# Where the gate row of layer 1's experts is applied, and the order of the last combine

## The chip, the cores and the metric

The kernel runs on one core of a Trainium2 chip. The metric is the time of one execution on the device, in microseconds (us). The program is given three times, and the median counts. The engines are PE (TensorE: matmuls, and PEld for its weight loads), DVE (VectorE), ACT (ScalarE), POOL (GpSimd) and SP (SyncE, which issues transfers here). Each works through its own instructions in order, and semaphores hold them against each other.

## What is computed

The model has an attention block, then a second block of two layers, each with a mixer and a mixture of experts. The change concerns the experts of the last layer, layer 1. There are 512 token rows of 1024 numbers (`h`, normed and modulated), 16 experts (4 groups of 4) with 256 hidden columns, and each token goes to two experts. Cut to what matters:

```python
def hier_moe(h, wg, bg, we, be, w_gate, w_up, w_down):
    ...                                   # combine: weights of the two chosen experts of each token
    for g in range(MOE_GROUPS):
        a = jnp.einsum('nd,edf->nef', h, w_gate[g])
        u = jnp.einsum('nd,edf->nef', h, w_up[g])
        hid = jax.nn.silu(a) * u * combine[:, g, :, None]
        out = out + jnp.einsum('nef,efd->nd', hid, w_down[g])
    return out
...
f_l = hier_moe(modulate(x, norm_ffn[i], mod_l[3], mod_l[4]).reshape(B * S, D), *moe_p)
x = x + mod_l[5] * f_l.reshape(B, S, D)
```

`mod_l[5]` is a row of 1024 numbers, the same for every token: the gate. Everything is fp32.

## The kernel before

`moe` runs a layer's experts. For layer 1 `n` is 4 (four tiles of 128 tokens). Each expert is a block `b` of up to `CAP` = 96 token rows; an expert with more rows would need further blocks, which stand in a branch (`tc.If`, label `rest1`, line 1974) that all engines jump over here.

**One block** (`block`, from line 1809). POOL gathers the token rows from DRAM by an indirect DMA (line 1780, tile `xg`). PE transposes them (`tr`, line 201); ACT rounds the result to `xhi` and DVE takes the rest `xlo` (line 157). The expert's weights come as six tiles of 128x1024 (512 KB each, tile `wraw`), which SP loads (line 138). Each tile is split in two: ACT casts it to `whi` (line 145) and DVE subtracts to get `wlo` (line 146). Every product is three matmuls, `whi` by `xhi`, `wlo` by `xhi` and `whi` by `xlo` (`mm3`, lines 151 to 153). Four tiles make `gu`, the gate and up products, from which ACT and DVE make `hd` (lines 1840, 1841); it is transposed and split, and two tiles make the two 512-wide halves of the output in PSUM (`yo`). These two halves are multiplied by the gate on DVE (line 1860, `y<-yo,g`). POOL scatters `y` to DRAM (line 1790): `yD` has two rows for each token, one for each of its two experts. In layer 0, `n` is 6, the blocks have 128 rows, there is no gate in `block`, and ACT copies `yo` to `y` (line 1858) instead.

**The order.** Blocks are interleaved by `run`: a block's transposes and first products are written between the parts of the block before. `prepare` puts a gather two blocks ahead, and with it `index_expert` (lines 1762 to 1772), DVE and PE work that finds the rows of that block. The tile framework then orders each engine's instructions by priority and dependence. The weight tiles turn through a ring of 25 buffers (14 + 4 + 7), so a load waits until the split of the tile 25 places earlier is done. `y` has 2 buffers, `yo` 2, the split tiles 4.

**The last two blocks** (`LAST`, 14 and 15) are not scattered. Their gated `y` is split into `hi` and `lo` in two `wraw` buffers (line 157, `wraw<-y`), and PE adds them to the tokens by a 0/1 matrix `sh` (`product`, lines 2015 and 2016, tile `yb`). Rows of `yD` that only these blocks would write are set to zero early: ACT makes a zero `y` (line 2006), and POOL scatters it twice.

**The end.** `run(None, None)` and `end()` finish blocks 14 and 15. SP loads the first rows of `yD` for four token tiles, and POOL adds the second rows in four accumulating DMAs (line 2045). DVE then adds `yb` to the residual `x` (line 2052, `X<-X,yb`) for two tiles, adds their `ys` (line 2055), and does the same for the other two; `finish` stores each 512-wide half from ACT's queue (line 130).

Of the kernel before, what the change touches and what calls it, by code (L numbers as in the profile page):

```python
# [8 lines left out]
F32 = mybir.dt.float32  # L9
# [5 lines left out]
OP = mybir.AluOpType  # L15
# [4 lines left out]
P = 128  # L20
# [875 lines left out]
class Fill:  # L896
# [10 lines left out]
    def finish(self):  # L907
        for _ in self.todo:
            pass
# [494 lines left out]
def row_bcast(K, st, pool, l, r, m, name):  # L1404
    t = pool.tile([P, D], F32, name=name, tag=name)
    K.load(t, st["dram"][l][r:r + 1, m * D:(m + 1) * D].to_broadcast([P, D]))
    return t
# [300 lines left out]
def moe(K, st, l, toks, mo, keep, first_ring, finish):  # L1708


    tc, nc, small, io, V = K.tc, K.nc, K.small, K.io, K.nc.vector
    n = len(toks)
# [4 lines left out]
    LAST = range(NLAST[l], 16)  # L1717
# [10 lines left out]
    pp = K.pool(es, "moep", PSUM)  # L1728
    yD = K.dram.tile([n * P, 2, D], F32, name="yD%d" % l)
# [9 lines left out]
    def source(e, i):  # L1739
        return io["ew"][l, e, i] if isinstance(e, int) else io["ew"][l, bass.ds(e, 1), i].rearrange("o p c -> (o p) c")  # L1740

    def fetch(m):
        for _ in range(min(m, len(chunks))):
            b, i = chunks.pop(0)
            ready[b, i] = K.fetch(source(expert[b], i))
# [37 lines left out]
    ysc, back, gate = [], [], None  # L1783
    half = (slice(0, 512), slice(512, 1024))
    if n == 4:
        gate = row_bcast(K, st, ex, l, toks[0][2], 5, "g5")

    def scatter(b, y):
        c = y.shape[0]
        sc = nc.gpsimd.indirect_dma_start(out=yD.rearrange("t k d -> (t k) d"),  # L1790
                                          out_offset=bass.IndirectOffsetOnAxis(ap=idx[:c, b:b + 1].bitcast(U32), axis=0),
                                          in_=y, in_offset=None, bounds_check=2 * n * P - 1, oob_is_err=False)
        for o in ysc:
            tc.declare_no_dep(sc.ins, o.ins, reason="other rows")
        ysc.append(sc)

    def block(b, e, xg):

        c = CAP if b < 16 else P
        xg = xg[:c]  # L1800
        xT = [ex.tile([P, KT, P], F32R, name=q, tag=q, bufs=2)[:, :, :c] for q in ("xhi", "xlo")]
        for k0 in range(0, KT, 4):
            tp = pp.tile([P, 512], F32, name="tr", tag="tr", bufs=2)
            for k in range(4):
                K.transpose(tp[:, k * c:(k + 1) * c], xg[:, (k0 + k) * P:(k0 + k + 1) * P])
            done = K.split(xT[0][:, k0:k0 + 4], xT[1][:, k0:k0 + 4], tp[:, :4 * c].rearrange("p (k q) -> p k q", k=4))

        def split(k):

            q, i = flow[k]  # L1810
            with ExitStack() as b_es:
                for x in done if q == 0 and i >= HOLD0 else ():
                    b_es.enter_context(tc.issue_after(x.ins))
                parted[q, i] = K.halves(ready.pop((q, i)))
            fetch(1)

        def weights(i):

            if b not in expert:
                K.load(xgs[2], source(e, i))  # L1820
                K.split(*spare, xgs[2])
                return spare
            k = flow.index((b, i))
            for q in range(k, min(k + 1 + SPLIT_AHEAD, len(flow))):
                if flow[q] not in parted:
                    split(q)
            return parted[b, i]

        yield
        gu = pp.tile([P, 512], F32, name="gu", tag="gu", bufs=2)[:c]  # L1830
        for kp in range(4):
            if kp == 2:
                yield
            hi, lo = weights(kp)
            for j in range(2):
                k = 2 * kp + j
                K.mm3(gu, (xT[0][:, k], xT[1][:, k]), (hi[:, j * 512:(j + 1) * 512], lo[:, j * 512:(j + 1) * 512]),
                      k == 0, k == KT - 1)
        hd = ex.tile([P, 256], F32, name="hd", tag="hd", bufs=2)[:c]
        nc.scalar.activation(hd, gu[:, :256], AF.Silu)  # L1840
        V.scalar_tensor_tensor(hd, hd, wsl[:c, b:b + 1], gu[:, 256:], op0=OP.mult, op1=OP.mult)
        yield
        tp = pp.tile([P, 512], F32, name="tr", tag="tr", bufs=2)
        for k in range(2):
            K.transpose(tp[:, k * c:(k + 1) * c], hd[:, k * P:(k + 1) * P])
        hT = [ex.tile([P, 2, P], F32R, name=q, tag=q, bufs=2)[:, :, :c] for q in ("hhi", "hlo")]
        K.split(hT[0], hT[1], tp[:, :2 * c].rearrange("p (k q) -> p k q", k=2))
        yield
        y = ex.tile([P, D], F32, name="y", tag="y", bufs=2)[:c]
        for ch in range(2):  # L1850
            hi, lo = weights(4 + ch)
            ps = pp.tile([P, 512], F32, name="yo", tag="yo", bufs=2)[:c]
            for j in range(2):
                K.mm3(ps, (hT[0][:, j], hT[1][:, j]), (hi[:, j * 512:(j + 1) * 512], lo[:, j * 512:(j + 1) * 512]),
                      j == 0, j == 1)
            cc = slice(ch * 512, (ch + 1) * 512)
            if gate is None:
                nc.scalar.copy(y[:, cc], ps)  # L1858
            else:
                V.tensor_tensor(y[:, cc], ps, gate[:c, cc], op=OP.mult)  # L1860
        if b not in LAST:
            return scatter(b, y)
        sh = token_rows(b, c)
        if gate is None:
            hi, lo = [K.wsp.tile([P, D], F32R, name=nm, tag=nm)[:c] for nm in ("whi", "wlo")]
        else:
            hi, lo = [K.raw(F32R)[:c] for _ in range(2)]
        for cc in half:
            K.split(hi[:, cc], lo[:, cc], y[:, cc])
        back.append((sh, hi, lo))  # L1870

    def token_rows(b, c):

        tok = small.tile([P, 1], F32, name="sk", tag="sk", bufs=2)[:c]
        V.tensor_copy(tok, xidx[:c, b:b + 1])
        V.tensor_scalar(tok, tok, -2048.0, None, op0=OP.add)
        at = small.tile([P, 8], F32, name="sa", tag="sa", bufs=2)[:c, :n]
        V.tensor_scalar(at, K.tile256[:c, :n], -0.5, tok, op0=OP.mult, op1=OP.add)
        sh = (K.wsp if gate is None else ex).tile([P, KT * P], F32R, name="sh", tag="whi" if gate is None else "xhi",
                                                  bufs=None if gate is None else 2)  # L1880
        sh = sh.rearrange("p (k q) -> p k q", q=P)[:c, :n]
        V.tensor_tensor(sh, K.iota[:c, None, :].to_broadcast([c, n, P]), at[:, :, None].to_broadcast([c, n, P]),
                        op=OP.is_equal)
        return sh
# [3 lines left out]
    def run(b, e, xg=None):  # L1888


        new = block(b, e, xg) if b is not None else None
        for x in (new, behind.pop(0) if len(behind) > 1 else None, new, behind[0] if behind else None, new):
            if x is not None:
                next(x, None)
        if new:
            behind.append(new)

    def end():
        next(behind.pop(), None)
# [112 lines left out]
    def product(t, psums):  # L2012
        for ps, cc in zip(psums, half):
            for i, (sh, hi, lo) in enumerate(back):
                nc.tensor.matmul(ps, sh[:, t], hi[:, cc], start=i == 0, stop=False)
                nc.tensor.matmul(ps, sh[:, t], lo[:, cc], start=False, stop=i == len(back) - 1)

    if n == 6:
        g5, ys = {}, {}
# [20 lines left out]
        es.close()  # L2040
        return load, combine
    run(None, None)
    ys = {t: K.fetch(yD[t * P:(t + 1) * P, 0]) for t, x, r in toks}
    for t, x, r in toks:
        nc.gpsimd.dma_start(ys[t], yD[t * P:(t + 1) * P, 1], accum_op=OP.add)
    end()
    for p in range(0, n, 2):
        for t, x, r in toks[p:p + 2]:
            psums = [pp.tile([P, 512], F32, name="yb", tag=tag, bufs=2) for tag in ("yo", "gu")]
            product(t, psums)  # L2050
            for ps, cc in zip(psums, half):
                V.tensor_add(x[:, cc], x[:, cc], ps)  # L2052
        for t, x, r in toks[p:p + 2]:
            for cc in half:
                V.tensor_add(x[:, cc], x[:, cc], ys[t][:, cc])  # L2055
                finish(t, x, cc)
    es.close()
    K.rings = base

# [339 lines left out]
def body(nc, tc, io, out, stop=None, skip1=False, force_slow=False):  # L2399
    with ExitStack() as es:  # L2400
# [79 lines left out]
        h_es.close()  # L2480
        a_es.close()
        back = moe(K, st, 0, toks, mo, keep, ring, None)
        if stop == "xb0":
            dump(X, C)
# [34 lines left out]
```

## Time and profile before

| | |
|---|---|
| three runs, median (lowest to highest) | 1970.19 us (1966.07 to 1971.62) |
| the profiled execution | 1971.35 us |
| its span, first to last instruction | 1969.5 us |
| mean granted TensorE clock | 0.947 |
| PE, PEld, DVE busy over the span | 91%, 70%, 71% |
| ACT, POOL busy over the span | 49%, 18% |
| layer 1's experts, from the branch to the end | about 1758 to 1969.5 us |

A time in the rows further down is us from the first instruction. A line of a timeline gives the start, the length, the engine, the line, the operation and the tiles (written<-read); `x2` merges two in a row. In square brackets stands how long the engine was idle before it, and what ended the wait. A matmul's end is modelled, so a busy PE is not PE at its peak. A line of waits says which instruction waited for which, with the sum, the count and the longest wait.

### The profile page before, as it was taken

The numbers are of one execution on the slowest core, as the hardware profiler recorded it, in microseconds if no ns is written. First come the engines' busy times: TensorE is split into PE (matmuls) and PEld (weight loads), VectorE is DVE, ScalarE is ACT, GpSimd is POOL, SyncE is SP. The second block draws the span as 40 slices with busy tenths as digits, with TensorE's granted clock in tenths as the row PEclk, the third lists the DMA queues.
The fourth block names the chain that finished last, engine by engine and source line by source line (L and its number), as shares of the span: only waits on it lengthen the run. The fifth ranks groups of instructions, "written<-read, shape, count | busy, mean of one in ns | idle before, by whom it ended". The sixth has DMA issues, their size and how long they took to land. (4 is left out here: it accounts for less than half of the span.)

```text
span 1969.5 us, 27283 instructions
## 1 busy us (share of the span) xinstructions
PE 1787.4 (91%) x9504; PEld 1371.1 (70%) x9504; DVE 1401.3 (71%) x2764; ACT 969.6 (49%) x1855; POOL 358.7 (18%) x301
## 2 busy tenths in 40 slices
PE   6999999899999997899989999699969799968996
PEld 5779766777777777576766778467737677755664
DVE  4554665677677767766567735799967978469997
ACT  4664476522222335522336812578846578336663
POOL 1010021000000010030131122133212311215651
PEclk9999999999999998797999998699979899979999
DMA  6423221565555545554110163699763100638985
GB/s 232 129 64 124 70 63 59 188 216 177 182 178 175 181 135 156 192 161 156 59 44 1 44 226 129 226 338 348 280 180 99 43 1 23 247 133 306 329 279 140
DMA packets 99674, 310.85 MB, mean 158 GB/s; under 512 B 17712, under 2 KB 21424, under 8 KB 99520
## 3 DMA queue, kind: packets, MB, share of 16 engines
q1 hardware_dynamic: 77952, 262.74, 40.3%
q0 software_dynamic: 10496, 27.58, 4.6%
q10 hardware_dynamic: 11072, 18.63, 2.6%
q8 instruction: 78, 1.28, 0.3%
q14 instruction: 76, 0.62, 0.1%
HBM read 287.25 MB, written 32.38 MB: 162 GB/s over the span
## 5 line engine op out<-in xcount | busy, mean ns | idle before, releaser
L145 ACT CAST whi<-wraw 128x1024 fp32r<-128x1024 f32 (+1 forms) x345 | 359.1, 1045 | 412.5 <-PE acc L152 138.7
L146 DVE TENSOR_TENSOR wlo<-wraw,whi 128x1024 fp32r<-128x1024 f32 (+1 forms) x345 | 410.6, 1214 | 95.2 <-ACT whi L145 87.7
L153 PE MATMUL acc<-ahi,wlo 128*128 128x512 f32 (+1 forms) x576 | 215.1, 374 | 3.7 <-DVE wlo L146 3.7
L151 PE MATMUL acc<-ahi,whi 128*128 128x512 f32 (+1 forms) x576 | 215.7, 376 | 2.7 <-DVE ss L176 1.7
L152 PE MATMUL acc<-alo,whi 128*128 128x512 f32 (+1 forms) x576 | 215.5, 374 | 0.0
L722 DVE SCALAR_TENSOR_TENSOR macc<-wraw,silu,macc 128x1024 f32<-128x1024 f32 x168 | 211.0, 1301 | 0.7 <-DMA wraw<-mod_w 0.7
L201 PE MATMUL tr<-ident,sc 128*128 128x128 f32 x752 | 125.3, 283 | 5.8 <-ACT sc L390 2.2
L151 PEld LDWEIGHTS acc<-ahi,whi 128*128 128x128 f32 x576 | 109.4, 190 | 26.5 <-ACT fhi L157 3.4
L153 PEld LDWEIGHTS acc<-ahi,wlo 128*128 128x128 f32 x576 | 109.8, 191 | 23.2 <-DVE wlo L146 4.1
L152 PE MATMUL gu<-wlo,xhi 128*128 128x512 f32 (+1 forms) x264 | 111.6, 423 | 13.1 <-DVE wlo L146 11.8
L152 PEld LDWEIGHTS acc<-alo,whi 128*128 128x128 f32 x576 | 109.8, 191 | 18.6 <-issue 0.4
L151 PE MATMUL acc<-whi,ahi 128*128 128x512 f32 (+2 forms) x288 | 107.3, 374 | 7.0 <-DVEq L1245 5.5
L201 PEld LDWEIGHTS tr<-ident,sc 128*128 128x128 f32 x752 | 84.0, 141 | 41.6 <-issue 13.6
L151 PE MATMUL gu<-whi,xhi 128*128 128x512 f32 (+1 forms) x264 | 107.8, 408 | 2.9 <-ACT whi L145 2.3
L153 PE MATMUL gu<-whi,xlo 128*128 128x512 f32 (+1 forms) x264 | 106.9, 405 | 1.7 <-DVE xlo L157 1.7
L152 PE MATMUL acc<-wlo,ahi 128*128 128x512 f32 (+2 forms) x288 | 104.9, 365 | 0.0
L153 PE MATMUL acc<-whi,alo 128*128 128x512 f32 (+2 forms) x288 | 103.9, 364 | 0.0
L1780 POOL DMA_INDIRECT xg<-hD,xidx x33 | 75.2, 2280 | 156.5 <-PE yo L153 64.4
L1790 POOL DMA_INDIRECT yD<-y,idx x33 | 73.3, 2221 | 88.0 <-ACT y L1858 31.6
L937 POOL COPY rw<-rd 128x256 f32<-128x256 f32 x52 | 21.6, 416 | 319.0 <-DVE rd L450 133.7
L892 PE MATMUL sps<-Kh,Q 128*128 128x256 f32 (+2 forms) x208 | 72.0, 355 | 6.0 <-DVE mn L2177 4.5
L152 PEld LDWEIGHTS gu<-wlo,xhi 128*128 128x128 f32 (+1 forms) x264 | 47.7, 181 | 40.1 <-DVE wlo L146 28.5
(545 smaller groups left out, 4238.9 us busy)
## 6 DMA issues: line engine op xcount, KB each, us to landing
wraw<-ew SPq DMA_DIRECT2D x198, 512.0 KB
wraw<-mod_w SPq DMA_DIRECT2D x96, 512.0 KB
wraw<-w_gate SPq DMA_DIRECT2D x22, 512.0 KB
wraw<-w_up SPq DMA_DIRECT2D x22, 512.0 KB
wraw<-w_down SPq DMA_DIRECT2D x22, 512.0 KB
wraw<-w_s SPq DMA_DIRECT2D x16, 512.0 KB
wraw<-w_out SPq DMA_DIRECT2D x12, 512.0 KB
wraw<-yD SPq DMA_DIRECT2D x10, 512.0 KB
```

Source lines behind the costliest of these rows:

```text
L145: nc.scalar.copy(hi[:, :n], raw[:, :n])
L146: (eng or nc.vector).tensor_tensor(lo[:, :n], raw[:, :n], hi[:, :n].bitcast(F32), op=OP.subtract)
L151: mm(out, a[0], b[0], start=start, stop=False)
L152: mm(out, a[0], b[1], start=False, stop=False)
L153: mm(out, a[1], b[0], start=False, stop=stop)
L201: self.nc.tensor.transpose(out, src, self.ident[:n, :n])
L722: nc.vector.scalar_tensor_tensor(acc[:, r], w, sr, acc[:, r], op0=OP.mult, op1=OP.add)
L892: K.nc.tensor.matmul(ps, q, Kh[:, cols], start=True, stop=False)
L937: K.nc.gpsimd.tensor_copy(rw, r[:, :, :, None].to_broadcast([P, 2, 2, 64]))
L1780: return nc.gpsimd.indirect_dma_start(out=xg[:c], out_offset=None, in_=mo["hD"], bounds_check=n * P - 1, oob_is_err=False, in_offset=bass. ...
L1790: sc = nc.gpsimd.indirect_dma_start(out=yD.rearrange("t k d -> (t k) d"), out_offset=bass.IndirectOffsetOnAxis(ap=idx[:c, b:b + 1].bitcast ...
```

## The change

For all but the blocks in `LAST`, `block` no longer multiplies `yo` by the gate on DVE: ACT copies it, as in layer 0. What lies in `yD` is then ungated. At the end, each token tile's sum of its `yD` rows is multiplied by the gate on DVE before it is added to `x`. Tiles 0 and 1 get both rows by plain loads from SP into two `wraw` buffers each, and DVE adds them (line 2056 of the new kernel); tiles 2 and 3 keep the accumulating DMA. The products of `LAST` are added for all four tiles first.

```diff
-            if gate is None:
+            if gate is None or b not in LAST:
                 nc.scalar.copy(y[:, cc], ps)
             else:
                 V.tensor_tensor(y[:, cc], ps, gate[:c, cc], op=OP.mult)
...
     run(None, None)
-    ys = {t: K.fetch(yD[t * P:(t + 1) * P, 0]) for t, x, r in toks}
+    ys = {t: [K.fetch(yD[t * P:(t + 1) * P, i]) for i in range(2 if t < 2 else 1)] for t, x, r in toks}
+    for t, x, r in toks[2:]:
+        nc.gpsimd.dma_start(ys[t][0], yD[t * P:(t + 1) * P, 1], accum_op=OP.add)
+    end()
     for t, x, r in toks:
-        nc.gpsimd.dma_start(ys[t], yD[t * P:(t + 1) * P, 1], accum_op=OP.add)
-    end()
-    for p in range(0, n, 2):
-        for t, x, r in toks[p:p + 2]:
-            psums = [pp.tile([P, 512], F32, name="yb", tag=tag, bufs=2) for tag in ("yo", "gu")]
-            product(t, psums)
-            for ps, cc in zip(psums, half):
-                V.tensor_add(x[:, cc], x[:, cc], ps)
-        for t, x, r in toks[p:p + 2]:
-            for cc in half:
-                V.tensor_add(x[:, cc], x[:, cc], ys[t][:, cc])
-                finish(t, x, cc)
+        psums = [pp.tile([P, 512], F32, name="yb", tag=tag, bufs=2) for tag in ("yo", "gu")]
+        product(t, psums)
+        for ps, cc in zip(psums, half):
+            V.tensor_add(x[:, cc], x[:, cc], ps)
+    for t, x, r in toks:
+        y = ys[t][0]
+        for cc in half:
+            for z in ys[t][1:]:
+                V.tensor_add(y[:, cc], y[:, cc], z[:, cc])
+            V.tensor_tensor(y[:, cc], y[:, cc], gate[:, cc], op=OP.mult)
+            V.tensor_add(x[:, cc], x[:, cc], y[:, cc])
+            finish(t, x, cc)
     es.close()
     K.rings = base
```

The framework reorders some of it. In the middle of layer 1's experts, ACT's instructions for one block read (before, with `-`; after, with `+`):

```order
 L145 CAST whi<-wraw 128x1024
 L157 CAST xhi<-tr 128x4x96
-L145 CAST whi<-wraw 128x1024 x2
+L1858 COPY y<-yo 96x512
+L145 CAST whi<-wraw 128x1024
+L1858 COPY y<-yo 96x512
+L145 CAST whi<-wraw 128x1024
 L157 CAST hhi<-tr 128x2x96
 L157 CAST xhi<-tr 128x4x96
```

The two copies came in, one in front of a weight cast each. On DVE the same block loses its two multiplies:

```order
 L157 TENSOR_TENSOR xlo<-tr,xhi 128x4x96
-L146 TENSOR_TENSOR wlo<-wraw,whi 128x1024
-L1860 TENSOR_TENSOR y<-yo,g_18264 96x512
-L146 TENSOR_TENSOR wlo<-wraw,whi 128x1024
-L1860 TENSOR_TENSOR y<-yo,g_18264 96x512
-L146 TENSOR_TENSOR wlo<-wraw,whi 128x1024 x2
+L146 TENSOR_TENSOR wlo<-wraw,whi 128x1024 x4
 L157 TENSOR_TENSOR hlo<-tr,hhi 128x2x96
```

The four subtractions of weight tiles now follow one another. Ahead of the stage, around the branch, SP has before (`g` is the gate row, `zd` where it lies in DRAM; the branch body, which is jumped over, begins with the row after the last):

```order
L1910 TENSOR_LOAD total
L1910 ISA x2
L138 DMA wraw<-ew 128x1024 x6
L127 DMA g_18264<-zd_76 128x1024
L138 DMA wraw<-ew 128x1024 x2
L1974 COMPARE_AND_BRANCH
```

and after, with the jump's target behind the dots:

```order
L1910 TENSOR_LOAD total
L1910 ISA x2
L138 DMA wraw<-ew 128x1024
L1974 COMPARE_AND_BRANCH
...
L1974 UNCONDITIONAL_BRANCH x2
L138 DMA wraw<-ew 128x1024 x5
L127 DMA g_18264<-zd_76 128x1024
L138 DMA wraw<-ew 128x1024 x72
```

Seven weight loads and the gate row moved from in front of the branch to behind it. DVE's last instructions, from the last block's `hd` on, are before:

```order
L1841 SCALAR_TENSOR_TENSOR hd<-hd,wsl,gu 96x256
...
L157 TENSOR_TENSOR wraw<-y,wraw 96x512
L1882 TENSOR_TENSOR sh<-iota,sa 96x512
L2052 TENSOR_TENSOR X_10342<-X_10342,yb 128x512 x4
L2055 TENSOR_TENSOR X_10342<-X_10342,wraw 128x512 x4
L2052 TENSOR_TENSOR X_10342<-X_10342,yb 128x512 x4
L2055 TENSOR_TENSOR X_10342<-X_10342,wraw 128x512 x4
```

and after (2051 is `X<-X,yb`, 2056 adds the two loads, 2057 multiplies by the gate, 2058 adds to `x`):

```order
L1841 SCALAR_TENSOR_TENSOR hd<-hd,wsl,gu 96x256
L1860 TENSOR_TENSOR y<-yo,g_18264 96x512
L146 TENSOR_TENSOR wlo<-wraw,whi 128x1024
...
L2056 TENSOR_TENSOR wraw<-wraw 128x512
L1860 TENSOR_TENSOR y<-yo,g_18264 96x512 x2
L2057 TENSOR_TENSOR wraw<-wraw,g_18264 128x512
L157 TENSOR_TENSOR wraw<-y,wraw 96x512 x2
L2051 TENSOR_TENSOR X_10342<-X_10342,yb 128x512 x8
L2056 TENSOR_TENSOR wraw<-wraw 128x512 x2
L2057 TENSOR_TENSOR wraw<-wraw,g_18264 128x512 x2
L2058 TENSOR_TENSOR X_10342<-X_10342,wraw 128x512 x3
```

One sum and one multiply of tile 0 moved in front of the products' additions; eleven further such instructions, of the same three kinds, follow up to the end.

## Rows read from the trace of the kernel before

**Rows 1.** Busy time, clock and DMA by stretch (start:end, length, then as headed).
```profile
core 0: us, PE busy (x) PEld busy (x) DVE busy (x) ACT busy (x) POOL busy (x), PEclk, DMA share, GB/s
1757.80:1769.40 11.60, 7.25 (x28) 5.14 (x28) 5.37 (x16) 2.81 (x3) 1.80 (x2) 0.50 0.82 270
...
1801.80:1900.90 99.10, 92.38 (x452) 60.50 (x451) 96.61 (x173) 67.12 (x91) 68.04 (x19) 1.00 0.97 328
1900.90:1940.20 39.30, 38.18 (x180) 25.72 (x179) 38.76 (x50) 29.52 (x40) 7.60 (x5) 1.00 0.35 116
1940.20:1969.50 29.30, 13.25 (x54) 8.80 (x52) 19.45 (x37) 3.29 (x6) 3.65 (x4) 0.85 0.79 215
```
**Rows 2.** Timeline of DVE, one block of layer 1's experts, `hd` to `hd`.
```profile
1801.82 0.47 DVE L1841 SCALAR_TENSOR_TENSOR hd<-hd,wsl,gu 96x256 f32<-96x256 f32 x1
...
1803.76 0.22 DVE L1762 TENSOR_SCALAR idx<-ix 96x1 int32<-96x1 f32 x1 [0.28 <-PE ix L1760]
...
1805.69 0.68 DVE L1860 TENSOR_TENSOR y<-yo,g 96x512 f32<-96x512 f32 x1
1806.29 1.21 DVE L146 TENSOR_TENSOR wlo<-wraw,whi 128x1024 fp32r<-128x1024 f32 x1
1807.42 0.68 DVE L1860 TENSOR_TENSOR y<-yo,g 96x512 f32<-96x512 f32 x1
...
1812.83 0.47 DVE L1841 SCALAR_TENSOR_TENSOR hd<-hd,wsl,gu 96x256 f32<-96x256 f32 x1
```
**Rows 3.** Waits of SP and of PE, 1780 to 1900 us.
```profile
SPq L138 <- DVE wlo L146: 87.5, 52, 8.9
...
PE gu L152 <- DVE wlo L146: 5.3, 10, 0.6
```
**Rows 4.** The stretch view of two blocks of layer 0's experts.
```profile
1358.65:1369.51 10.86, 10.40 (x54) 7.82 (x53) 10.42 (x20) 8.80 (x13) 3.90 (x3) 1.00 0.99 365
...
1422.31:1431.68 9.37, 9.37 (x47) 7.76 (x46) 8.93 (x11) 8.55 (x13) 1.81 (x2) 1.00 0.30 112
```
**Rows 5.** Layer 0's copies on line 1858 (ns shortest/median/longest, first and last start).
```profile
L1858 ACT COPY y<-yo x34: 579/587/589, 1277.8 to 1443.5; 128x512 f32<-128x512 f32 x34
```
**Rows 6.** Timelines of SP, POOL and ACT about layer 1's branch.
```profile
1759.06 4.49 SPq L138 DMA_DIRECT2D wraw<-ew  x6
...
1758.74 1.17 POOL L1780 DMA_INDIRECT xg<-hD,xidx  x1 [0.30 <-ACTq L1974]
...
1769.45 1.04 ACT L2006 COPY y<-zero 128x1024 f32<-128x1024 f32 x1 [5.87 <-DMA wraw<-yD]
```
**Rows 7.** The branch's line 1974 in layer 1, SP's and POOL's events.
```profile
L1974 SPq EVENT_SEMAPHORE  x9: 17/17/17, 1771.2 to 1778.0; - x9
L1974 POOLq EVENT_SEMAPHORE  x4: 17/43/43, 1768.0 to 1768.2; - x4
```
**Rows 8.** Landing times of the gathers `xg`, 1755 to 1940 us.
```profile
DMA to landing us min/median/max: 4.7/9.6/12.3
```
**Rows 9.** Timelines of POOL and ACT about layer 0's branch.
```profile
1243.99 1.17 POOL L1780 DMA_INDIRECT xg<-hD,xidx  x1 [0.30 <-issue]
...
1251.88 1.04 ACT L2006 COPY y<-zero 128x1024 f32<-128x1024 f32 x1 [2.70 <-remote]
```
**Rows 10.** Timelines of DVE and PE at the end.
```profile
1940.16 0.47 DVE L1841 SCALAR_TENSOR_TENSOR hd<-hd,wsl,gu 96x256 f32<-96x256 f32 x1
...
1950.84 2.48 DVE L2052 TENSOR_TENSOR X<-X,yb 128x512 f32<-128x512 f32 x4 [0.89 <-PE yb L2016]
...
1963.32 2.49 DVE L2055 TENSOR_TENSOR X<-X,wraw 128x512 f32<-128x512 f32 x4
...
1955.54 0.39 PE L2016 MATMUL yb<-wraw,sh 96*128 96x512 f32 x1
```
**Rows 11.** Waits of DVE, 1936 to 1971 us.
```profile
DVE X L2055 <- DMA wraw<-yD: 5.1, 2, 3.9
```
**Rows 12.** Landing times of the scatters of `y`, 1755 to 1950 us.
```profile
DMA to landing us min/median/max: 4.3/10.1/10.9
```

## The prediction

> **What bounds the kernel now.** I read the stretch view first, since a mean over the span mixes stages. Layer 1's experts have four of them here [rows 1]. In the nine steady blocks (1801.8 to 1900.9 us, 11.01 us each) DVE is busy 96.6 of 99.1 us, PE 92.4 and the DMA engines 0.97 of the time. In the four late blocks (to 1940.2, 9.82 us each, no index work and few transfers) DVE has 38.76 and PE 38.18 of 39.30. Three resources that all look full call for the waits. SP's weight loads wait for a `wlo` to free a ring buffer, 87.5 us in 52 waits, the longest 8.9, and PE's `gu` products wait 5.3 us for DVE's `wlo` [rows 3]. So transfers wait for DVE and not DVE for transfers: the DMA share of 0.97 is a queue kept full ahead of its need. DVE's own timeline then shows what it does in a block [rows 2]: from `hd` at 1801.82 to `hd` at 1812.83 the one wait is 0.28 us for PE's `ix`. DVE sets the period, PE is close behind.
>
> Layer 0 shows what a block looks like whose `y` ACT copies, for it has that form already, with 128 rows where layer 1 has 96. A steady block there takes 10.86 us with DVE 10.42 and PE 10.40, and one without index work 9.37 us with PE busy 9.37 and DVE 8.93 [rows 4]: without index work PE is the bound.
>
> **The change part by part.** The sum is made against the profiled run of 1971.35 us.
>
> *The multiplies, steady blocks.* Each block loses two. One lasts 0.68 us, but the next instruction starts 0.60 later (1805.69 to 1806.29), so 1.2 us of DVE go per block [rows 2]. DVE's busy time falls from 96.61/9 = 10.73 to 9.53 us. Where does the period stop? By DVE: layer 0's period exceeds its DVE time by 10.86 - 10.42 = 0.44 [rows 4], which gives 9.97. By PE: 9.37 for a block without index work [rows 4], plus what index work adds, 92.38/9 - 38.18/4 = 10.26 - 9.55 = 0.72 [rows 1], gives 10.09. The bounds are 9.53 (DVE without any wait) and 10.72 (PE's present 10.26 taken as all work, plus the 0.46 by which layer 0's period exceeds PE's busy time). I take PE's 10.09, the later of the two middle values: 0.92 per block, **-8.3** over nine (-13.3 to -2.6).
>
> The copies go to ACT, two of 0.587 us per block [rows 5]. ACT is busy 67.12/9 = 7.46 us per block; with 1.17 more it has 8.63 of about 10, as in layer 0, where it has 8.80 of 10.86 [rows 1, 4]. That room hides them; without it they would cost their 1.17 us. They stand in front of weight casts, so a late `yo` would hold a cast and then DVE's `wlo`. Layer 0 has the same order and its DVE is still busy 96%.
>
> *The multiplies, block 0.* It lies between the start and the steady stretch, where DVE also waits for other things. Two multiplies are 1.2 us; I take half, **-0.6** (-1.2 to 0).
>
> *The multiplies, late blocks.* DVE falls from 38.76/4 = 9.69 to 8.49, so PE is late next, at layer 0's 9.37 or a little less, since transposes of 96 rows are shorter than those of 128. At 9.37 the gain is 0.45 per block, **-1.8** for four (-3.3 with DVE's 8.49 plus 0.5 for waits; 0 if PE's 9.55 were all work and DVE's present 0.13 us of idle time stayed with the overlap lost).
>
> *The branch.* Before, SP issues six loads in one row from 1759.06 on [rows 6], then the gate row and two more, and at the branch it waits for its transfers: nine events, from 1771.2 to 1778.0 [rows 7]. POOL waits there for its gather: issued 1758.74, its events at 1768.0 [rows 6, 7]. ACT's zero `y`, which waited 5.87 us, starts at 1769.45, 10.71 us after the gather's issue [rows 6]. The clock in this stretch is 0.50, the low level, and the DMA share 0.82 [rows 1]. After the change one load stands before the branch, as in layer 0, where the same steps take 1251.88 - 1243.99 = 7.89 us [rows 9]. The gather then shares the queues with one load in place of eight, and 10.71 - 7.89 = 2.8 us go. Against it, the first weights behind the branch are issued later: the five loads and the gate row that now follow it. PE has its transposes and `xhi` to do first, which hides most of that, and a cover that is gone would take back what was gained. SP itself is free at the branch once one load has landed, where it was held until 1778.0. I take **-2.5** (0 to -4.5; the far end is a gather at the fastest landing, 4.7 against 9.3 us here [rows 6 to 8]).
>
> Beside this the Trainium skill, "Advanced Engine Details and Errata", Control Flow Timing, puts a compare-and-branch at some 108 ns. SP's events here last until 1778.0, so the row shows that what precedes the branch, and not the jump, costs the time; by the page's figure alone this part would be worth nothing and the sum 2.5 us less.
>
> *The tail.* From the last block's `hd` at 1940.16 to the end of DVE's last addition at 1963.32 + 2.49 = 1965.81 it takes 25.65 us now [rows 10], with 5.1 us of waits for the accumulating loads [rows 11] and 0.89 for PE's `yb` [rows 10]. The change adds twelve 512-wide instructions: eight multiplies by the gate and four sums of two loads. At 2.49/4 = 0.62 us each [rows 10] that is 7.5 us. Against it stand the 5.1 of waits, because all eight `X<-X,yb` now come before the last three tiles' loads are needed, and 0.9. That is 7.5 - 6.0 = +1.5. But two of these, tile 0's sum and gate multiply, stand ahead of `X<-X,yb`, where DVE partly waits for PE: PE's `yb` went on until 1955.9 with DVE in step [rows 10], and now runs through without the pause between the pairs, so some of DVE's work is hidden: 0.7 back. The other way, that first sum stands in front of the last `y` multiplies, and if tile 0's loads land late (the present 3.9 us wait is the longest for such a load [rows 11]) DVE is held there and PE's products behind it: half a microsecond on average. Sum **+1.3** (-1 to +4). The 3.7 us from DVE's end to the span's end, the last stores, stay.
>
> *Sum.* -8.3 - 0.6 - 1.8 - 2.5 + 1.3 = -11.9, so 1959.4 for a run like the profiled one. The median of the three runs lies 1.2 below that run: **1958.2 us**.
>
> **The rivals.**
>
> *DMA is the bound (0.10).* For: a share of 0.97 in the steady blocks; 328 GB/s x 11.01 us = 3.61 MB per block, and at 328/0.97 = 338 GB/s that needs 10.68 us. The nine blocks would gain 3.0 us in place of 8.3, and the total is -6.6: 1963.5. Against: no weight load is waited for, and layer 0 reached 365 GB/s [rows 4], at which the block needs 9.89 us, less than PE. On this the Trainium skill, "DMA: Bandwidth & Descriptors", names about 358 GB/s of HBM as one core's share and notes that a core running alone gets more; layer 0's row stands a little above that share and so agrees with the second. By the page's 358 a block would need an estimated 10.1 us, and the sum would be the same within half a microsecond.
>
> *PE is the bound already (0.10).* For: PE is busy 92.4 of 99.1 us, and layer 0's block, with the copies on ACT, still takes 10.86. At the 10.72 worked out above nine blocks gain 2.6, and if the late blocks and the start gain nothing and the tail costs 1.3, the total is -1.3 to -3: about 1968, no measurable change. Against: a matmul's end is modelled, so stalls within a run of matmuls count as busy, and `gu` waits for `wlo` in the waits [rows 3].
>
> *ACT is held by the scatters (0.04), slower.* `y` has two buffers, so ACT's copy of block b waits until the scatter of block b-2 has landed, and the casts behind it in ACT's queue wait with it. DVE's multiply had the same wait, but the next casts could run ahead. A scatter lands 10.1 us after its issue in the median and 10.9 at most [rows 12]; from the buffer's first writing it is wanted again two periods later, 20 us. So it decides when a landing takes more than some 17 us, with 3 us for copy and issue. If the fuller queues did that, and cost 1.7 us a block, the steady period would be 10.09 + 1.7 = 11.8, 7 us above now in nine blocks, and with the rest -3.6: 1974, and beyond 1976 at 2 us. Against it: landings are at little more than half of that.
>
> **How the numbers follow.** The forecast has 0.76. A run of this kernel can tell about 0.3%, 5.9 us, from no change. Faster by more is under 1964.3: the forecast but for a tenth of its weight, and two thirds of the DMA case, in all 0.76. Within 0.3%: what is left of these two, the PE case, and half of the last one, 0.22. Slower: 0.02. The range reaches from 1951, where the steady blocks run at DVE's 9.6 and the branch gives 4, up to 1966, which takes in the DMA case and a tail of +4 but not PE's; some 0.08 is left out below and 0.12 above.
>
> **What would show each step right or wrong.** Steady `hd` to `hd` near 10.1 us, with DVE and PE both at 95% or more, shows the first; 10.7 with loads that wait for no `wlo`, or casts that wait for a load, shows DMA; 10.7 with PE free of waits shows PE; ACT's copy waiting for a transfer of `y` shows the scatters. Late blocks near 9.4 with PE full show the third. ACT's zero `y` some 8 us behind the first gather shows the branch, and a first `gu` that waits for a weight load would show the gain given back. For the tail it is `hd` to the last addition, near 27 us, with no wait for an accumulating load; a wait of the first sum for a load would make it longer. The prediction is wrong as a whole if the steady period stays above 10.6.

## The result and the profile after

The changed kernel is slower: 1980.74 us in the median of five runs (1979.18 to 1985.36), against 1967.28 us (1965.78 to 1971.62) for the kernel before. The ratio is 1.0064, with a 95% interval of 1.0045 to 1.0083, and the forecast was 1958.2 us. Ratios here and below are of fast runs alone; one run of 6312.39 us, of the variant with the new end alone, is outside them. The profiled run took 1985.36 us, with a span of 1983.6.

I cut both traces at the same events: the first gather, `hd` of block 2, of block 11 and of block 15 (DVE, line 1841), and the end. The stretch view of before, cut so (columns as in [rows 1]):

```profile
1757.32:1801.82 44.50, 31.75 (x152) 21.57 (x153) 32.30 (x82) 24.62 (x32) 16.47 (x8) 0.82 0.84 290
1801.82:1900.89 99.07, 92.35 (x452) 60.47 (x451) 96.58 (x173) 67.09 (x91) 68.04 (x19) 1.00 0.97 328
1900.89:1940.16 39.27, 38.15 (x179) 25.72 (x178) 38.73 (x50) 29.49 (x40) 7.60 (x5) 1.00 0.35 116
1940.16:1969.53 29.37, 13.29 (x54) 8.82 (x52) 19.49 (x37) 3.33 (x6) 3.65 (x4) 0.85 0.79 214
```

and the changed kernel's:

```profile
1756.56:1798.89 42.33, 30.58 (x150) 21.85 (x151) 31.42 (x80) 25.17 (x34) 14.93 (x7) 0.75 0.85 299
1798.89:1917.38 118.49, 97.59 (x452) 68.17 (x451) 87.46 (x153) 76.99 (x109) 68.30 (x21) 0.88 0.85 291
1917.38:1954.63 37.25, 37.25 (x183) 26.60 (x182) 36.50 (x49) 33.61 (x48) 11.82 (x5) 1.00 0.28 84
1954.63:1983.56 28.93, 12.94 (x53) 8.45 (x51) 24.52 (x41) 2.84 (x6) 1.91 (x2) 0.80 0.67 212
```

| stage | before | after | difference | predicted |
|---|---|---|---|---|
| start, to `hd` of block 2 | 44.50 | 42.33 | -2.2 | -3.1 |
| nine steady blocks | 99.07 | 118.49 | **+19.4** | -8.3 |
| four late blocks | 39.27 | 37.25 | -2.0 | -1.8 |
| end | 29.37 | 28.93 | -0.4 | +1.3 |

The steady blocks alone turned the result. DVE is busy for 9.1 us less (the forecast took away 9 x 1.2 = 10.8), yet idle for 31 us; the clock there fell from 1.00 to 0.88 and the DMA share from 0.97 to 0.85. Every resource is busy for a smaller share of the time, so something was waited for. The periods alternate: from block 2 on 16.01, 9.86, 14.81, 9.85, 16.52, 9.85, 15.58, 9.86 and 16.16 us. The shorter ones are better than the 10.09 of the forecast.

PE's timeline in a slow block shows the hole, in front of the transposes of the gathered rows:

```profile
1827.76 0.33 PE L201 MATMUL tr<-ident,hd 96*128 96x96 f32 x2
1831.70 0.58 PE L201 MATMUL tr<-ident,xg 96*128 96x96 f32 x4 [3.62 <-DMA xg<-hD,xidx]
```

and that block in four stretches shows what the hole costs behind it:

```profile
1824.76:1828.09 3.33, 3.33 (x19) 2.14 (x17) 3.25 (x11) 3.18 (x5) 2.15 (x3) 1.00 0.93 360
1828.09:1831.67 3.58, 0.00 (x0) 0.00 (x0) 3.58 (x4) 1.37 (x3) 3.58 (x1) 1.00 0.99 358
1831.67:1835.50 3.83, 3.80 (x13) 2.65 (x14) 0.52 (x2) 1.48 (x2) 2.03 (x2) 0.55 1.00 386
1835.50:1839.57 4.07, 4.07 (x22) 2.92 (x21) 2.46 (x3) 2.56 (x5) 0.00 (x0) 1.00 0.86 311
```

PE stands still for 3.58 us, then runs for 3.83 us at 0.55 of its clock, about the lower of its two levels (1.2 and 2.4 GHz). The waits of 1780 to 1910 us (engine, line, released by: sum, count, longest):

```profile
PE tr L201 <- DMA xg<-hD,xidx: 12.2, 3, 4.6
...
PE tr L201 <- DVE hlo L157: 4.2, 1, 4.2
PE tr L201 <- DVE wlo L146: 3.8, 1, 3.8
```

Five waits, 20.2 us, one for each slow block. The two that name DVE name the instruction that happened to end last before them (in one case an `hlo` that ends at 1856.87, for transposes that start at 1857.01): in the block shown above, the same transposes start at 1831.70, ahead of the `hlo` at 1831.84, so they do not need it. The gather is late. Its landing times, beside [rows 8]:

```profile
DMA to landing us min/median/max: 7.2/14.0/14.4
```

Of the 4.4 us by which the median rose, 4.0 pass on POOL, in the instruction that issues the gather (7.69 us for 3.72). The profile's spans on POOL are rough, but landings and PE's waits say the same. POOL's timeline before (a gather on line 1780, a scatter on line 1790):

```profile
1815.89 3.72 POOL L1780 DMA_INDIRECT xg<-hD,xidx  x1 [3.29 <-PE tr L201]
1819.92 3.67 POOL L1790 DMA_INDIRECT yD<-y,idx  x1 [0.30 <-issue]
```

after:

```profile
1817.80 7.69 POOL L1780 DMA_INDIRECT xg<-hD,xidx  x1 [9.62 <-PE yo L152]
1825.79 0.97 POOL L1790 DMA_INDIRECT yD<-y,idx  x1 [0.31 <-DVE oh L1772]
1827.63 5.14 POOL L1780 DMA_INDIRECT xg<-hD,xidx  x1 [0.87 <-PE yo L152]
```

and what DVE does meanwhile:

```profile
1817.48 4.62 DVE L146 TENSOR_TENSOR wlo<-wraw,whi 128x1024 fp32r<-128x1024 f32 x4
1822.01 0.35 DVE L157 TENSOR_TENSOR hlo<-tr,hhi 128x192 fp32r<-128x192 f32 x1
1822.28 2.35 DVE L146 TENSOR_TENSOR wlo<-wraw,whi 128x1024 fp32r<-128x1024 f32 x2
1824.76 0.48 DVE L1841 SCALAR_TENSOR_TENSOR hd<-hd,wsl,gu 96x256 f32<-96x256 f32 x1
```

An instruction that takes 0.97 us where nothing disturbs it takes 7.69 while DVE runs `wlo` after `wlo`, and ends 0.86 us after the last of them (1824.63 to 1825.49). In the kernel before the two multiplies stood between the subtractions, and it took 3.72.

### The profile page after: what moved, and what is told of

Same layout as the page of the kernel before. It is cut to its first block, busy times and chain, and to the rows that moved or that the text cites. A ratio compares the mean times of both kernels' runs of the same rounds, so it can differ in the third digit from the quotient of the medians.

```text
span 1983.6 us, 27293 instructions
## 1 busy us (share of the span) xinstructions
PE 1787.4 (90%) x9504; PEld 1377.3 (69%) x9504; DVE 1393.4 (70%) x2748; ACT 984.3 (50%) x1883; POOL 361.1 (18%) x299
## 5 line engine op out<-in xcount | busy, mean ns | idle before, releaser
L1780 POOL DMA_INDIRECT xg<-hD,xidx x33 | 102.3, 3099 | 177.2 <-PE yo L153 64.4
L153 PE MATMUL gu<-whi,xlo 128*128 128x512 f32 (+1 forms) x264 | 111.0, 421 | 3.0 <-DVE xlo L157 3.0
L201 PE MATMUL tr<-ident,xg 128*128 128x128 f32 (+1 forms) x264 | 40.0, 282 | 39.0 <-DMA xg<-hD,xidx 19.1
L971 POOL TENSOR_TENSOR xs<-X,gf 128x1024 f32<-128x1024 f32 x2 | 4.8, 2399 | 371.9 <-DVE X L631 371.9
```

The source lines that it names most:

```text
L153: mm(out, a[1], b[0], start=False, stop=stop)
L201: self.nc.tensor.transpose(out, src, self.ident[:n, :n])
L971: (V if late else nc.gpsimd).tensor_tensor(y, x, gf, op=OP.mult)
L1780: return nc.gpsimd.indirect_dma_start(out=xg[:c], out_offset=None, in_=mo["hD"], bounds_check=n * P - 1, oob_is_err=False, in_offset=bass. ...
```

## The experiments

Three theories, as the expectations name them. **1:** DVE's uninterrupted `wlo` holds POOL's gather. **2:** the copies stand ahead of the weight casts in ACT's queue and hold them. **3:** the DMA queues are fuller, and the transfers late for that. All times below are medians beside runs of the kernel before on the same chip. The profiled runs differ by up to 12 us ahead of the stage, where no variant changes the work (the first gather starts between 1746.36 and 1758.51), so stages are counted from the first gather.

### Both copies on DVE

```diff
-            if gate is None or b not in LAST:
+            if gate is None:
                 nc.scalar.copy(y[:, cc], ps)
+            elif b not in LAST:
+                V.tensor_copy(y[:, cc], ps)
```

> The changed kernel with the two copies of y on DVE in place of ACT; branch and tail as in the changed kernel. Theory 1 (held gather): with y copied from PSUM on DVE between the wlo subtractions, POOL's gather instruction is short again, 3.7 us instead of 7.7 and 5.1, it lands some 9.6 us after its issue, PE's wait for xg (3.6 us in every second block) goes, and the steady period is 11.0 us. Total: the kernel before, plus the start's +1.65 and the tail's -0.4, about 1969. Theory 2 (ACT's queue: the copies stand ahead of casts and hold them): also about 1969, since ACT has no copies left. Theory 3 (the transfers are late because the DMA queues are fuller at the shorter blocks): the gathers still land late, 12 to 14 us after the issue, and the period stays above 12.

1968.33 against 1967.85 us, ratio 1.001 (0.9986 to 1.0033). The gathers are back at their old length, and the period at 11.0 us:

```profile
1821.28 3.72 POOL L1780 DMA_INDIRECT xg<-hD,xidx  x1 [3.27 <-PE tr L201]
1825.30 3.67 POOL L1790 DMA_INDIRECT yD<-y,idx  x1 [0.30 <-issue]
```

So neither the new branch order nor the new end makes the gathers late, for both are in this kernel. Theories 2 and 3 are still open, since ACT has no copies here and the blocks are no shorter than before. The run also gives the price of those two parts: the start to `hd` of block 2 takes 43.78 us (44.50 before) and the end 31.35 (29.37), together +1.3.

### The gathers one block earlier

```diff
-    xgs = [ex0.tile([P, D], F32, name="xg%d" % i) for i in range(3)]
+    xgs = [ex0.tile([P, D], F32, name="xg%d" % i) for i in range(4 if n == 4 else 3)]
...
-MOE_RAW2 = ((5, 4, 2), (7, 0, 0))
+MOE_RAW2 = ((5, 4, 2), (6, 0, 0))
...
-            prepare(GAHEAD - 1)
+            prepare(GAHEAD - 1 + (n == 4))
```

> The changed kernel with a fourth gather buffer and each gather one block earlier in the program; the load ring has 24 tiles in place of 25 for the room. Theory 1 (held gather): POOL's instruction may still take 5 to 8 us, but the landing comes before PE needs it; PE's wait for xg goes and the steady period is 9.9 to 10.3 us; total 1957 to 1962. Theory 2 (ACT's queue): the period keeps alternating, total 1978 to 1982. Theory 3 (DMA): the gathers are covered, but the weight loads would be late next, period 10.7 or more, 1964 or more.

1956.62 against 1967.85 us, ratio 0.9945 (0.9921 to 0.9969). Eight steady blocks, and two instructions of POOL in them:

```profile
1794.75:1873.62 78.87, 77.63 (x402) 54.61 (x401) 76.94 (x136) 68.02 (x97) 68.14 (x15) 1.00 0.99 359
```
```profile
1817.38 7.68 POOL L1780 DMA_INDIRECT xg<-hD,xidx  x1 [0.91 <-PE yo L152]
1825.37 0.97 POOL L1790 DMA_INDIRECT yD<-y,idx  x1 [0.30 <-DVE oh L1772]
```

The gather is held as long as ever, but nobody waits for it: 9.86 us a block, PE and DVE both 98% busy. ACT's order is that of the changed kernel, so theory 2 falls. 359 GB/s flow, so DMA was no bound at 328, and the weight loads that theory 3 held for late next are not. One late block took 14.24 us. ACT's timeline there shows the third rival of the prediction, at a single place:

```profile
1888.91 0.58 ACT L1858 COPY y<-yo 96x512 f32<-96x512 f32 x1 [4.78 <-DMA yD<-y,idx]
```

POOL had issued that scatter late, behind a gather of 8.28 us, and ACT's copy waited for its buffer with the casts behind it.

### The control: before, with the gathers one block earlier

The same three edits on the kernel before.

> The kernel before with the fourth gather buffer, the gathers one block earlier and the ring of 24 tiles: the control for that step without the copies on ACT. If the changed kernel with gathers ahead (1956.6) won because the copies on ACT pay once the gathers are covered, this one stays at the kernel before, 1965 to 1969, with the steady period at 11.0 us. If most of the gain was the earlier gathers themselves, it comes out at 1957 to 1961.

1959.92 against 1966.61 us, ratio 0.9966 (0.9946 to 0.9985): the second of the two cases, not "stays at the kernel before". But it is not won in the steady blocks, which take 10.99 us (eight of them):

```profile
1792.90:1880.81 87.91, 81.98 (x402) 53.84 (x401) 85.79 (x154) 59.53 (x81) 60.55 (x17) 1.00 0.97 330
```

Index work ends a block earlier, so five blocks in place of four run at 9.76 us, worth 1.25, and the end takes 26.65 us in place of 29.37. From the first gather to the end it takes 208.7 us in place of 212.2: 3.5 of the 6.7 us. Where the rest lies the traces do not show. So only part of the last experiment's gain comes from the copies on ACT. In the steady block, though, these two kernels differ by nothing else, and there the copies are worth 10.99 - 9.86 = 1.13 us, once the gather is covered. Of these 9.0 us in eight blocks 3.7 are left at the end, by the profiled runs (205.0 us from the first gather for 208.7): the end of the kernel with the copies on ACT takes 31.0 us for 26.65, and its late blocks, with the one of 14.24 us, 1.3 us more.

### Without the subtractions

`no_lo` is set in layer 1's `moe`. The kernel leaves out the low half of the weights; PE multiplies by `whi` a second time in its place.

```diff
+        if self.no_lo:
+            return hi, hi
         (eng or nc.vector).tensor_tensor(lo[:, :n], raw[:, :n], hi[:, :n].bitcast(F32), op=OP.subtract)
```

> The changed kernel without the wlo subtractions of layer 1's experts: PE multiplies by whi in their place, so PE's, ACT's and the transfers' work is the same, and DVE has 6 x 1.2 us per block less to do (this leaves out the low half of the weights, and its time is that of a kernel with less work). If it is DVE's wlo that holds POOL's instruction (theory 1): gathers and scatters of 0.95 to 1.3 us throughout, landing within 10 us, no wait of PE for xg, steady period at PE's 9.4 to 9.9 us. If something else holds it, the DMA queues or POOL itself: gathers stay at 4 us or more, and PE still waits for xg in every second block.

One run, 1950.04 us, against 1964.49 us, with less work to do. With the copies on ACT as in the changed kernel and the same transfers (DMA share 1.00), but no `wlo` (lines 1784 and 1794 are its gather and scatter):

```profile
1817.72 0.98 POOL L1784 DMA_INDIRECT xg<-hD,xidx  x1 [5.17 <-PE tr L204]
1820.98 0.93 POOL L1794 DMA_INDIRECT yD<-y,idx  x1 [2.28 <-ACT y L1862]
```
```profile
1798.20:1873.15 74.95, 74.95 (x403) 54.21 (x401) 22.67 (x87) 66.44 (x97) 15.30 (x16) 1.00 1.00 352
```

All held instructions are free: it is `wlo` that holds POOL. Theory 3 falls here, for the steady blocks are the shortest of all, the DMA engines are busy throughout (share 1.00), and yet PE waits for no gather. The period is 9.37 us with PE busy all the time.

On this the Trainium skill, "SBUF — State Buffer", SBUF: two separate sides, says that transfers issued by GpSimd have their descriptors written by its cores, and that these are locked out of a port shared with DVE while DVE holds it, so that the transfer seems blocked. Among what takes that port it names DVE operations with two SBUF inputs, as `wlo` has, though only against a GpSimd operation that reads SBUF. The 0.98 against 7.68 us agrees, and it is the rule that spoke against this change; that it is this port that holds POOL no run here shows.

### What lets the gather through

Five variants of the changed kernel ask how much interruption is needed. Two have one half copied by DVE, the other by ACT (`ch == 0`, then `ch == 1`):

```diff
+            if gate is not None and b not in LAST and ch == 0:
+                V.tensor_copy(y[:, cc], ps)
-            if gate is None or b not in LAST:
+            elif gate is None or b not in LAST:
```

> The changed kernel with the first of the two copies on DVE, the second on ACT. In the run with 64-column copies on DVE the gather stayed long, so gaps of 0.05 to 0.2 us between wlo do not release it; in the kernel before, gaps of 0.52 us did, and the gather ended 0.5 us after the second. Theory 1a (a gap of about half a microsecond releases it, but one that comes in its first 0.9 us is too early): gathers stay at 7.7 to 8.3 and 5.1 to 5.7 us, PE still waits for xg, total 1978 to 1986. Theory 1b (any such gap is enough): gathers end by 2.5 us after their start, steady period 10.4 us, total 1961 to 1965. ACT's order as the cause (theory 2): half of the copies gone, so about half of the loss, 1974.

> The changed kernel with the second of the two copies on DVE, the first on ACT. Theory 1a (a gap of half a microsecond that comes after the gather's first 0.9 us releases it): gathers of 2.5 to 3.7 us, PE does not wait for xg, steady period 10.4 us, total 1961 to 1965. Theory 1c (the gather needs both gaps): gathers stay at 5 to 8 us, total 1978 to 1986. Theory 2 (ACT's order): about 1974, as in the run with the first copy on DVE.

One has DVE copy 64 columns of each half, ACT the other 448:

```diff
+            elif b not in LAST:
+                nc.scalar.copy(y[:, cc][:, 64:], ps[:, 64:])
+                V.tensor_copy(y[:, cc][:, :64], ps[:, :64])
```

> The changed kernel, ACT copying 448 of the 512 columns of each half and DVE the other 64, so that DVE has a short instruction on PSUM at each place where the multiply stood, and ACT's copies stay ahead of the casts. Theory 1 (held gather): the short instructions break the run of wlo, the gather's instruction falls to about 3.7 us, PE no longer waits for xg, and the steady period is 10.1 to 10.5 us; total 1958 to 1964. Theory 2 (ACT's queue): ACT's order is unchanged, so 1978 to 1982 and the alternating periods of 9.9 and 15 to 16 us stay. Theory 3 (DMA): likewise unchanged.

One cuts each `wlo` into two of 512 columns (`parts` is set in layer 1's `moe`):

```diff
-        (eng or nc.vector).tensor_tensor(lo[:, :n], raw[:, :n], hi[:, :n].bitcast(F32), op=OP.subtract)
+        for sl in self.parts or [slice(0, n)]:
+            (eng or nc.vector).tensor_tensor(lo[:, sl], raw[:, sl], hi[:, sl].bitcast(F32), op=OP.subtract)
```

> The changed kernel with each wlo subtraction of layer 1's experts as two of 512 columns: the same columns, twice as many ends at which POOL may go on, and some 0.06 us per instruction more on DVE, 0.4 us a block. If the held instruction goes on at a wlo's end and only needs more of them: gathers of 3 to 4.5 us, alternation gone or small, total 1962 to 1972. If it takes a longer stretch in which DVE does no wlo, whatever the number of ends: gathers stay at 5 to 8 us, total 1982 to 1992.

And one has both copies on DVE, one right behind the other:

```diff
+            elif b not in LAST:
+                held.append((cc, ps))
...
+        for cc, ps in held:
+            V.tensor_copy(y[:, cc], ps)
```

> The changed kernel with both copies of y on DVE, as in the run that restored the gathers, but one right behind the other, so that DVE does no wlo for one stretch of about 1.1 us in place of two of 0.52. If a stretch of about 0.9 us without wlo lets the held gather through (in every held gather so far the end came 0.85 us after the last wlo before such a stretch): gathers of 3 to 3.5 us, period 11.0, total 1965 to 1970. If it takes two separate gaps: gathers of 5 to 9 us, PE waits for xg, total 1990 or more.

| variant | gathers, us | time, us | before, us | ratio (95%) |
|---|---|---|---|---|
| first half on DVE | 8.29 and 5.74 | 1995.44 | 1966.61 | 1.0163 (1.0136 to 1.0191) |
| second half on DVE | 8.31 and 5.74 | 2002.3 | 1966.61 | 1.0209 (1.0178 to 1.0241) |
| 64 columns of each | 7.96 and 5.40 | 1987.92 | 1967.85 | 1.0106 (1.0081 to 1.0132) |
| two `wlo` for one | 8.15 and 5.42 | 1994.83 | 1964.49 | 1.014 (1.0109 to 1.017) |
| both on DVE, together | 3.72 | 1965.68 | 1970.76 | 0.9983 (0.9963 to 1.0003) |

A gather of each, POOL's timelines in the table's order, one kernel to a fence:

```profile
1811.93 8.29 POOL L1780 DMA_INDIRECT xg<-hD,xidx  x1 [9.89 <-PE yo L153]
```
```profile
1813.78 8.31 POOL L1780 DMA_INDIRECT xg<-hD,xidx  x1 [9.40 <-PE tr L201]
```
```profile
1807.39 7.96 POOL L1780 DMA_INDIRECT xg<-hD,xidx  x1 [8.14 <-PE tr L201]
```
```profile
1821.89 8.15 POOL L1783 DMA_INDIRECT xg<-hD,xidx  x1 [10.64 <-PE tr L203]
```
```profile
1818.94 3.71 POOL L1780 DMA_INDIRECT xg<-hD,xidx  x1 [3.30 <-PE tr L201]
```

My theory 1 in its first form, that any short instruction between two `wlo` lets the gather through, is wrong: the 64-column copies did nothing and cost DVE time. So are the finer forms by which one gap of 0.52 us is enough: it was not at either of the two places tried. Nor do twice as many ends help. One stretch of 1.1 us without `wlo`, or two of 0.52, does shorten layer 1's gathers. But the reason that I gave for the last run beforehand, an end 0.85 us after the last `wlo`, is not what DVE's timeline shows there:

```profile
1818.62 2.35 DVE L146 TENSOR_TENSOR wlo<-wraw,whi 128x1024 fp32r<-128x1024 f32 x2
1820.89 1.28 DVE L1865 COPY y<-yo 96x512 f32<-96x512 f32 x2
1822.09 2.35 DVE L146 TENSOR_TENSOR wlo<-wraw,whi 128x1024 fp32r<-128x1024 f32 x2
```

The gather ended at 1822.65, 1.68 us after the second `wlo` and 0.56 us into the third. By the Trainium skill's page named above the port is held for the whole of one instruction; here the hold went on over the ends of eight halved instructions in a row, so that does not describe all of it. With one half on DVE the kernel is worse than with both: it pays for a copy and keeps the hold. In the first of these two the late scatters were held too, 5.96 us, and the end took 39.4 us.

What ends a hold was not settled. In the kernel before, the scatters of the steady blocks take 3.67 us under `wlo` with only an `hlo` between. And in layer 0 of the same kernel four `wlo` follow one another as in the changed one:

```profile
1302.76 4.62 DVE L146 TENSOR_TENSOR wlo<-wraw,whi 128x1024 fp32r<-128x1024 f32 x4
1302.92 1.95 POOL L1780 DMA_INDIRECT xg<-hD,xidx  x1 [6.65 <-PE yo L153]
```

That gather ends at 1304.87, some 0.9 us after the end of the one `wlo` that it began in (1302.76 + 1.21), while the next one runs. It waited for one instruction, where layer 1's waited for six or four; so a stretch without `wlo` is not always needed. Layer 0's gathers have 128 rows and begin 0.16 us into a `wlo`, those of layer 1 96 rows and 0.32 us; no run tells whether one of these is the reason.

### The new end alone

The kernel before with the new end, without the gate multiplies there.

> The kernel before with the new end alone: products first, plain loads for two tiles, no gate at the end since block still applies it on DVE. The steady blocks stay at 11.0 us and the gathers at 3.7. The end takes 25.65 us now; 6.0 of waits go, four sums come at 0.62: about 22 to 23 us, total 3 us below the kernel before, 1965. A rival: the waits for the loads stay because the sums wait for their plain loads, and the end is unchanged within 1 us.

1965.7 against 1967.85 us, ratio 0.9975 (0.9954 to 0.9996). The start and the end of the stage in the profiled run:

```profile
1752.35:1801.13 48.78, 36.16 (x151) 24.75 (x152) 32.41 (x81) 24.51 (x32) 13.99 (x8) 0.72 0.79 266
...
1939.88:1966.90 27.02, 13.55 (x54) 8.72 (x52) 21.90 (x41) 3.32 (x6) 1.91 (x2) 0.89 0.75 233
```

The end takes 27.02 us in place of 29.37, as the first theory had it (-2.35 for about -3). But in this run the start to `hd` of block 2 took 48.78 us in place of 44.50, and the stage from the first gather 214.55 in place of 212.18. So the trace shows the gain of the end alone; where the small gain of the total lies, and why this start was longer, it does not show.

### Gathers ahead and a third buffer for `y`

On the kernel with the gathers ahead, with a ring of 23 (the zero `y` has the same number of buffers):

```diff
-        y = ex.tile([P, D], F32, name="y", tag="y", bufs=2)[:c]
+        y = ex.tile([P, D], F32, name="y", tag="y", bufs=3 if n == 4 else 2)[:c]
```

> The changed kernel with gathers ahead and a third y buffer, the load ring at 23 tiles. In the run with two y buffers one block took 14.2 us since ACT's copy waited 4.8 us for a scatter that POOL had issued late behind a gather of 8.3 us. With three buffers that wait goes: that block at 9.5, total 1951 to 1954. If the shorter ring holds the loads back, the steady period rises above 9.9 and the total is 1957 or more.

1951.65 against 1966.61 us, ratio 0.9929 (0.9897 to 0.996): the lowest of the kernels that do all the work, though its interval overlaps that of the kernel with two `y` buffers (0.9921 to 0.9969). The late block that took 14.24 us takes 9.70, and the steady ones are as fast:

```profile
1794.14:1872.89 78.75, 77.57 (x402) 54.60 (x401) 76.92 (x136) 68.00 (x97) 69.82 (x17) 1.00 0.99 361
```

## Why the prediction was wrong

**What bounds the kernel.** Right: DVE set the period of 11.01 us, PE was close behind, and the queue of weight loads was no bound.

**The multiplies, steady blocks.** The step that failed is "Where does the period stop?": the prediction let only DVE and PE stop it, between 9.53 and 10.72 us, and put PE's wait for the gathered rows at nothing without a reason. The runs showed 118.49/9 = 13.17 us a block in its place, with 20.2 us of PE's waits for `xg`, since the gather was held on POOL. The multiplies had a second effect, which no row on DVE shows: they interrupted `wlo` for POOL. The trace of before held both halves of the hint. POOL was busy 68.04 us with 19 instructions, 3.6 us each, where single ones took 1.17 [rows 1, 6]; I read no cause for that. And the gather landed 9.6 us after its issue [rows 8], and PE's waits in the steady blocks had this line (sum, count, longest):

```profile
PE tr L201 <- DMA xg<-hD,xidx: 0.5, 2, 0.3
```

Two of those gathers kept PE waiting already, so there was no slack to lose. Landing at 14.0 us in place of 9.6 put 20.2 us of waits in front of PE's transposes. The rest of the slow blocks' excess over the fast 9.86, 29.8 - 20.2 = 9.6 us, came with it; the low clock behind each hole has a part in it, for PE's busy time rose from 92.35 to 97.59 us with the same 452 matmuls.

"That room hides them", of the copies on ACT, held: with the gathers covered the period is 9.86 us with both copies on ACT, where I took 10.09 between bounds of 9.53 and 10.72. Layer 0's excess of 0.44 over DVE gave the nearer of my two middle values (9.97), in part by luck, for two errors cancel: DVE was busy for 9.62 us a block, not 9.53, and the excess was 0.24, not 0.44.

**Layer 0 as a model.** It was right for the period and wrong for the gather. There, too, four `wlo` follow one another, yet the gathers take 1.95 us. Two stages with DVE's instructions in the same order are not the same for POOL.

**The late blocks.** Right: 37.25 us for four, -2.0 for -1.8, PE busy all the time.

**The branch and block 0.** The size was nearly right, -2.2 for -3.1, the way there not. ACT's zero `y` came earlier, 8.8 us after the second gather (1757.98) in place of 10.7:

```profile
1766.76 1.04 ACT L2006 COPY y<-zero 128x1024 f32<-128x1024 f32 x1 [6.48 <-DMA wraw<-yD]
1767.70 0.85 ACT L157 CAST xhi<-tr 128x384 fp32r<-128x384 f32 x2
```

but both `xhi` stand behind it now, one of which stood ahead, so `hd` of block 0 came 22.81 us after the first gather in place of 21.16. What was won came in the two blocks behind it, 19.52 us in place of 23.34. The run with both copies on DVE, without block 0's multiplies removed, won 0.7 us there.

**The end.** -0.4 for +1.3, and +2.0 in the run with both copies on DVE; the range of -1 to +4 holds both. From the last `hd` to DVE's last addition it is now 25.17 us:

```profile
1954.63 0.46 DVE L1841 SCALAR_TENSOR_TENSOR hd<-hd,wsl,gu 96x256 f32<-96x256 f32 x1
...
1979.11 0.69 DVE L2058 TENSOR_TENSOR X<-X,wraw 128x512 f32<-128x512 f32 x1
```

The multiplies were paid for by the waits that went, as the sum had it: over the whole end DVE is busy for 24.52 us in place of 19.49 and idle for 4.41 in place of 9.88. And one `wlo` less stands behind that `hd` than before, 1.2 us that the sum did not see.

**The rivals.** DMA as the bound and PE as the bound were both refuted by the 9.86 us. The scatters as a brake came true once, in another kernel, and for a reason of POOL's; the slower case that happened is a sibling of it, the gather instead of the scatter, held on POOL instead of in the queue. I had given all of "slower" 0.02. Two small sums are off without touching the forecast: the chances of 0.76 and 0.22 come to 0.75 and 0.23 by their own terms, and the low end of the range, by the terms named for it, to some 1952 us in place of 1951.

## What to carry to other kernels

Before work is taken from an engine, ask who profits from what it interrupts: a longer run of the same instruction can hold another engine. An instruction of POOL that takes 3.7 us in one place and 1 us in another is a sign of such a hold, and the first thing to look up is how long before its use its transfer lands. Where the hold can't be removed, issue the transfer a block earlier: that turned a loss of 0.6% into a gain of 0.5%, and with a third output buffer of 0.7%. Then run the same step on the kernel before as well: there it gained 0.3% by itself.

## What the runs showed of the hardware

While DVE runs fp32 subtractions of two SBUF tiles back to back, an indirect DMA issued by POOL takes up to 8.3 us in place of 0.98. In layer 1 the hold does not end with the DVE instruction that is running: it outlasted eight ends in a row in one run, gaps of 0.05 to 0.2 us, and one of 0.52 us. A stretch of 1.1 us of copies from PSUM, or two of 0.52, cut it to 3.7. In layer 0, under the same four subtractions, a gather waited for one of them only and took 1.95 us. And a hole of 3.6 us in PE's work was followed by 3.8 us at 0.55 of its clock.
